# Two-layer hybrid decoder on one core: the MLP's order written down for all engines one step ahead, its first 1024 features multiplied plainly, PSUM banks in two kinds

## The chip, the cores and the metric

The kernel runs on one core of one Trainium2 chip. The metric is the device time of one execution in microseconds (us). A core has TensorE (PE) for matmuls and transposes, VectorE (DVE), ScalarE (ACT) and GpSimd (POOL) for the rest, and SyncE (SP), which here does nothing but issue transfers of weights. Matmuls write into PSUM, which has eight banks of 128 partitions x 2 KB (one 128x512 fp32 tile each).

## The reference

256 tokens of width 2048 go through two layers. Each layer normalizes, projects to queries, keys, values and memory queries, does attention (layer 0 differential, layer 1 dilated in three groups) and attention over 256 memory tokens, projects out and adds, and then runs a squared-ReLU MLP:

```python
hm = _rmsnorm(x, g_mlp[i])
x = x + jnp.square(jax.nn.relu(hm @ w_mlp1[i])) @ w_mlp2[i]   # 2048 -> 8192 -> 2048
```

All is fp32. A final RMSNorm ends it.

## The kernel before

**Products.** A product of two fp32 matrices is made of three passes: each operand is split into hi (ACT, L114) and lo (DVE, L115, source minus hi), and PE adds hi·hi, hi·lo and lo·hi in one PSUM bank. Each weight tile (512 KB, 128 partitions x 1024 fp32) so costs one transfer on SP's queue (L82), one ACT and one DVE instruction of 1024 wide. `weights` (L106 to L117) does that with three buffers for raw tiles (RAW = 3) and four each for hi and lo.

**Stages of a layer.** Attention comes first: `gemm_feat` (queries and keys, two heads at a time, L126) is followed by scores, softmax parts on DVE and ACT and transposes (`tp`, L428) of these two heads; then `project_v` (`psv`) and `mix_out` (L534: `o`, `os`, transposes `op`, L558). Then comes the output projection (`pso`, L577 to L589), which also makes, chunk by chunk, the combined activations of the MLP (`to_comb`, L186), and then the MLP.

**The MLP.** The 8192 features are 8 blocks of 1024. Up: with two halves of the tokens, two halves of a 256-row slice of the weights and two halves of the block's features it is a 2x2 times 2x2 product, done by Winograd's seven products instead of eight. A step of it is one of 8 row slices (`kp`): `up_weights` (L207) loads two tiles b and o (L220, L222), makes from them the seven weight factors (s, o and t sums on DVE at L227, L229, L230, splits on ACT and DVE), and 21 matmuls (L602 to L604) add to seven banks p1 to p7. After eight steps one ACT and seven DVE instructions (L621 to L628) put the seven banks together, and Relu and Square (L630, L631) make `u`. `to_hT` (L635) transposes u (`pu`, L642, four tiles of four transposes) and splits it into hT. Down: `mlp_down` (L651) has 4 column pieces n with four weight tiles (`raw_d`) each, and for each of two token halves t a group of 24 matmuls into one bank `psd` (L669 to L671); ACT scales it to `part` (L674) and POOL adds it to x in SBUF by an accumulating DMA (L675). The last block of a layer adds on DVE (L677) instead; in layer 0 it also transposes the new x for the next layer (`to_feat`, `pt_xa`, L176).

**What sets the order.** In the MLP PE's order is written by hand (`manual_schedule` for PE alone): first all of block 0's up steps and one of block 1; then for each block c, hT of c within up step 1 of block c+1, and the eight down groups of c, each followed by an up step of c+1 (the last by step 0 of c+2). Everything else (ACT, DVE, SP, POOL in the MLP, and all engines outside it) is ordered by a planner that simulates the program.

**PSUM banks.** `bank` (L72 to L74) has two tags: "u" of 7 banks in rotation, for all gemms, for scores, transposes and the seven products; and "d", one bank, for `pu` and `psd` of the MLP.

Of the kernel before, what the change touches and what calls it, by code (L numbers as in the profile page):

```python
# [9 lines left out]
F32 = mybir.dt.float32  # L10
# [7 lines left out]
P = 128  # L18
S = 256
D = 2048  # L20
KT = D // P
# [18 lines left out]
PRODUCTS = ("p1", "p2", "p4", "p5", "p6", "p3", "p7")  # L40
# [18 lines left out]
def trunk(ctx: ExitStack, tc: tile.TileContext, x, mem, g_attn, w_in, w_out, lambda_qk,  # L59
# [10 lines left out]
    psum = ctx.enter_context(tc.tile_pool(name="psum", bufs=7, space=bass.MemoryType.PSUM))  # L70
# [31 lines left out]
    pw = bank([P, 512], "pw")  # L102
# [23 lines left out]
    def gemm_feat(w, acts, nm, raws=(None,) * 4):  # L126

        ps = [bank([P, 2, 256], f"ps_{nm}_{j}") for j in range(2)]
# [57 lines left out]
    def to_comb(kp, gcol, nm):  # L186
# [3 lines left out]
        for a in range(2):  # L190
            k = 2 * kp + a
            for t in range(2):
                nc.tensor.transpose(pt[:, a, t, :], x_sb[:, t, k * P:(k + 1) * P], ident)
            nc.scalar.activation(xs[:, a], pt[:, a], AF.Copy, scale=gT[:, gcol + k:gcol + k + 1])
        cs = work.tile([P, 4, P], F32, tag="tmp", bufs=TMP, name=f"cs_{nm}")
        a11, a12, a21, a22 = xs[:, 0, 0], xs[:, 1, 0], xs[:, 0, 1], xs[:, 1, 1]
# [5 lines left out]
        cb = apool.tile([P, 7, 2, P], F32R, tag="act", name=f"cb_{nm}")  # L202
        for i0, i1, a in ((0, 2, xs[:, :, 0]), (2, 3, xs[:, 1, 1:2]), (3, 7, cs)):
            split(cb[:, i0:i1, 0, :], cb[:, i0:i1, 1, :], a)
        return cb

    def up_weights(w, kp, f0, nm):  # L207

# [13 lines left out]
        nc.sync.dma_start(o, pair(512, -512))  # L222
        b11, b22 = pieces(b, 2, "b")
        oh = upool.tile([P, 2, 512], F32R, tag="up", bufs=UP, name=f"oh_{nm}")
        split(oh[:, 0], oh[:, 1], o[:, 1])
        s = upool.tile([P, 2, 512], F32, tag="ut", bufs=UT, name=f"s_{nm}")
# [5 lines left out]
        return {"p1": b11, "p2": (oh[:, 0], oh[:, 1]), "p3": b22, "p5": t1, "p7": t3, "p6": t2, "p4": t4}  # L232
# [73 lines left out]
    def project_mem():  # L306
        mrstd = rstd_of(mssq, "mem")
        mrowb = bcast_row(mrstd, "mem")
        for i in range(DEPTH):
# [4 lines left out]
            ps = [bank([P, 512], f"psvm{i}_{t}") for t in range(2)]  # L314
# [120 lines left out]
    for i in range(DEPTH):  # L435
# [89 lines left out]
        def project_v(g):  # L525
            ps = [bank([P, 512], f"psv{i}{g}_{t}") for t in range(2)]
# [50 lines left out]
        for c in range(4):  # L577
            ps = [bank([P, 512], f"pso{i}{c}_{t}") for t in range(2)]
# [19 lines left out]
        turns = []  # L598

        def product(ps, n, kp, hi, lo):  # L600
            ah, al = (comb[kp][:, PRODUCTS.index(n), h, :] for h in range(2))
            nc.tensor.matmul(ps, ah, hi, start=kp == 0, stop=False)  # L602
            nc.tensor.matmul(ps, ah, lo, start=False, stop=False)  # L603
            nc.tensor.matmul(ps, al, hi, start=False, stop=kp == KP - 1)  # L604

        def mlp_up(c):


            nm = f"{i}{c}"
            ps = {n: bank([P, 512], f"{n}_{nm}") for n in ("p1", "p3", "p2", "p5", "p7", "p6", "p4")}  # L610
            for kp in range(KP):
                wt = up_weights(w_mlp1[i], kp, c * 1024, f"{nm}{kp}")
                for n in ps:
                    if turns and n in ("p1", "p3", "p5", "p6"):
                        next(turns[0])
                    product(ps[n], n, kp, *wt[n])
                if kp < KP - 1:
                    yield
            c1, u2, u3, u4 = (work.tile([P, 512], F32, tag="tmp", bufs=TMP, name=f"t{n}_{nm}") for n in range(4))
            c11, m12, c21, m22 = (work.tile([P, 512], F32, tag="ev", bufs=EV, name=f"u{n}_{nm}") for n in range(4))  # L620
            nc.scalar.activation(c1, ps["p1"], AF.Copy)  # L621
            nc.vector.tensor_tensor(u2, c1, ps["p6"], op=ALU.subtract)
            nc.vector.tensor_tensor(c11, c1, ps["p2"], op=ALU.add)
            nc.vector.tensor_tensor(u4, u2, ps["p5"], op=ALU.add)
            nc.vector.tensor_tensor(u3, u2, ps["p7"], op=ALU.add)
            nc.vector.tensor_tensor(m12, u4, ps["p3"], op=ALU.add)
            nc.vector.tensor_tensor(m22, u3, ps["p5"], op=ALU.add)
            nc.vector.tensor_tensor(c21, u3, ps["p4"], op=ALU.add)  # L628
            for u, sign in ((c11, 1.0), (m12, -1.0), (m22, -1.0), (c21, 1.0)):
                nc.scalar.activation(u, u, AF.Relu, scale=sign)  # L630
                nc.scalar.activation(u, u, AF.Square)  # L631
            ublk[c] = ((c11, 0, 0), (m12, 0, 1), (c21, 1, 0), (m22, 1, 1))
            yield

        def to_hT(c):  # L635
# [3 lines left out]
            for n, (u, t, f) in enumerate(ublk[c]):  # L639
                pt = bank([P, 4, P], f"pu_{i}{c}{n}", True)  # L640
# [6 lines left out]
        final = i == DEPTH - 1  # L647
        ssq = small.tile([P, 2, 4], F32, tag="ssq", name=f"ssq_e{i}")
        nxt = []

        def mlp_down(c):  # L651


            for n in range(3 if final and c == NC - 1 else 4):
                if final and c == NC - 1:
# [3 lines left out]
                wt = []  # L659
                xc = x_sb[:, :, n * 512:(n + 1) * 512]  # L660
                for t in range(2):
                    ps = bank([P, 512], f"psd{i}{c}{n}{t}", c < NC - 1)
                    for k in range(8):
                        r0 = c * 1024 + k * P
                        if k == len(wt):
                            wt += weights(w_mlp2[i][r0:r0 + 256, n * 512:(n + 1) * 512], 2, 512, f"d{i}{c}{n}{k}")
                        hi, lo = wt[k]
                        ah, al = (hT[k // 4][:, k % 4, h, t * P:(t + 1) * P] for h in range(2))
                        nc.tensor.matmul(ps, ah, hi, start=k == 0, stop=False)  # L669
                        nc.tensor.matmul(ps, ah, lo, start=False, stop=False)  # L670
                        nc.tensor.matmul(ps, al, hi, start=False, stop=k == 7)  # L671
                    if c < NC - 1:
                        part = work.tile([P, 512], F32, tag="tmp", bufs=TMP, name=f"part{i}{c}{n}{t}")
                        nc.scalar.activation(part, ps, AF.Copy, scale=rsq[:, t:t + 1])  # L674
                        nc.gpsimd.dma_start(xc[:, t, :], part, accum_op=ALU.add)  # L675
                    else:
                        nc.vector.scalar_tensor_tensor(xc[:, t, :], ps, rsq[:, t:t + 1], xc[:, t, :],  # L677
                                                       op0=ALU.mult, op1=ALU.add)
                    yield
                if c == NC - 1:  # L680
                    if not final:
                        xt = act_tile(f"xT{i + 1}_{n}")
                        to_feat(lambda t: x_sb[:, t, :], n, xt, (i + 1) * KT, f"xa{i}{n}")
                        nxt.append(xt)
                    for t in range(2):
                        sumsq(xc[:, t, :], ssq[:, t, n:n + 1])
                    if final:
                        for t in range(2):
                            nc.vector.tensor_tensor(xc[:, t, :], xc[:, t, :], gf, op=ALU.mult)

        with tc.manual_schedule(engines={mybir.EngineType.PE}):
            ups = [mlp_up(c) for c in range(NC)] + [iter(()), iter(())]
            for _ in ups[0]:
                pass
            next(ups[1])
            for c in range(NC):
                turns.append(to_hT(c))
                next(ups[c + 1], None)
                for _ in turns.pop():
                    pass  # L700
                for k, _ in enumerate(mlp_down(c)):
                    next(ups[c + 1] if k < 6 else ups[c + 2] if k == 6 else iter(()), None)
# [70 lines left out]
```

## Time and profile before

| | us |
|---|---|
| median of 3 runs | 2617.06 (2615.62 to 2618.43) |
| profiled execution, its own time | 2610.07 |
| its span in the trace | 2608.3 |

Times in rows are us from the start of the span. A row of a timeline gives the start, the duration, engine, line, operation, output and inputs by name; "x4" is four in a row; the bracket is the engine's idle time before it and what ended it. "Wait" rows sum such idle time by the pair of waiting and releasing line. PEclk is the granted TensorE clock as a share of full speed (2.4 GHz). Of a DMA, "to landing" is the time from its issue on the queue to its completion.

### The profile page before, as it was taken

Reading aid. Unit: us, or ns where it says so; the run is one execution under the profiler, and the core shown is the slowest. Engines: PE = TensorE matmul, PEld = TensorE weight load, DVE = VectorE, ACT = ScalarE, POOL = GpSimd, SP = SyncE. Lnnn points to the kernel's source line nnn. Section 1 sums busy time; section 2 is a strip of 40 time slices with the busy share of each in tenths; the row PEclk is TensorE's granted clock in tenths of the full one; section 3 lists DMA queues with packets and bytes.
Section 4 is the critical chain, followed back from the end, with each engine's and each line's share of the span. In section 5 each row is a group of like instructions: output and inputs, shape, how many; then the busy total and the mean of one; then the engine's idle time right before and its main releaser. Section 6 shows DMA issues by size and latency. Waiting matters only on the chain.

```text
span 2608.3 us, 28509 instructions
## 1 busy us (share of the span) xinstructions
PE 2294.7 (88%) x10310; PEld 1845.6 (71%) x10310; DVE 1780.9 (68%) x2194; ACT 1355.7 (52%) x1890; POOL 114.5 (4%) x146
## 2 busy tenths in 40 slices
PE   9977678698899999999977888989798999999997
PEld 7856556575678778777866677777477787787776
DVE  6544554468887888788754344456888878978874
ACT  6433333355565666566544333445456656656563
POOL 0000000000000000000000000000000000000000
PEclk9978788899999999999998888999999999999998
DMA  7633344454476667667644244555466766776664
GB/s 230 193 106 105 97 122 129 130 185 145 140 216 200 190 210 217 200 190 213 174 141 145 91 131 130 165 188 185 121 175 189 217 199 207 215 203 188 202 174 145
DMA packets 262400, 443.51 MB, mean 170 GB/s; under 512 B 14497, under 2 KB 80242, under 8 KB 262002
## 3 DMA queue, kind: packets, MB, share of 16 engines
q1 hardware_dynamic: 245856, 412.14, 50.3%
q0 software_dynamic: 16128, 29.37, 6.3%
q8 instruction: 81, 1.33, 0.2%
q14 instruction: 61, 0.50, 0.1%
q10 hardware_dynamic: 274, 0.17, 0.0%
HBM read 409.12 MB, written 3.15 MB: 158 GB/s over the span
## 4 chain that ended last, share of the span: by engine, by line
PE 39%; DVE 20%; DMA 13%; issue 7%; ACT 5%; POOL 0%; SPq 0%; DVEq 0%; POOLq 0%; ACTq 0%
DMA raw_d<-in_w_mlp_dram 6%; DMA o<-in_w_mlp_dram 6%; PE psd L669 4%; PE psd L670 4%; PE psd L671 3%; DVE lo_d L115 3%; PE p L602 3%; PE p L603 3%; PE p L604 3%; DVE b L230 2%; DVE b L229 2%; ACT hi_d L114 2%; DVE sl L115 2%; DVE bl L115 2%; PE ps_q L143 2%
## 5 line engine op out<-in xcount | busy, mean ns | idle before, releaser
L669 PE MATMUL psd<-hi_d,hT 128*128 128x512 f32 x1008 | 396.0, 393 | 8.0 <-DVE hT L115 6.4
L670 PE MATMUL psd<-lo_d,hT 128*128 128x512 f32 x1008 | 393.8, 391 | 1.0 <-DVE lo_d L115 1.0
L671 PE MATMUL psd<-hi_d,hT 128*128 128x512 f32 x1008 | 393.3, 390 | 0.0
L114 ACT ACTIVATE hi_d<-raw_d 128x1024 fp32r<-128x1024 f32 x252 | 260.2, 1053 | 198.8 <-DMA raw_d<-in_w_mlp_dram 104.6
L115 DVE TENSOR_TENSOR lo_d<-raw_d,hi_d 128x1024 fp32r<-128x1024 f32 x252 | 307.0, 1223 | 75.4 <-ACT hi_d L114 73.7
L114 ACT ACTIVATE th<-b 128x1024 fp32r<-128x1024 f32 x128 | 135.3, 1057 | 209.0 <-DVE b L230 198.4
L669 PEld LDWEIGHTS psd<-hi_d,hT 128*128 128x128 f32 x1008 | 190.2, 189 | 54.5 <-DVE hT L115 12.4
L670 PEld LDWEIGHTS psd<-lo_d,hT 128*128 128x128 f32 x1008 | 190.0, 188 | 40.5 <-DVE lo_d L115 1.7
L671 PEld LDWEIGHTS psd<-hi_d,hT 128*128 128x128 f32 x1008 | 189.9, 188 | 39.8
L115 DVE TENSOR_TENSOR bl<-b,bh 128x1024 fp32r<-128x1024 f32 x128 | 156.0, 1219 | 73.6 <-ACT bh L114 73.6
L227 DVE TENSOR_TENSOR s<-b,o 128x1024 f32<-128x1024 f32 x128 | 156.4, 1222 | 72.1 <-DMA o<-in_w_mlp_dram 71.3
L115 DVE TENSOR_TENSOR tl<-b,th 128x1024 fp32r<-128x1024 f32 x128 | 156.4, 1222 | 54.9 <-ACT th L114 54.0
L143 PE MATMUL ps_q<-xT,hi_q 128*128 128x512 f32 x384 | 158.5, 446 | 0.0
L115 DVE TENSOR_TENSOR sl<-s,sh 128x1024 fp32r<-128x1024 f32 x128 | 155.8, 1217 | 2.9 <-ACT sh L114 1.6
L675 POOL DMA_DIRECT2D x_sb<-part x112 | 97.3, 869 | 1333.7 <-ACT part L674 1322.7
L114 ACT ACTIVATE sh<-s 128x1024 fp32r<-128x1024 f32 x128 | 134.8, 1053 | 28.1 <-PE p L603 27.3
L114 ACT ACTIVATE bh<-b 128x1024 fp32r<-128x1024 f32 x128 | 135.0, 1054 | 26.7 <-PE p L603 24.5
L143 PE MATMUL ps_k<-xT,hi_k 128*128 128x512 f32 x384 | 136.2, 397 | 0.0
L115 DVE TENSOR_TENSOR lo_k<-raw_k,hi_k 128x1024 fp32r<-128x1024 f32 x48 | 58.7, 1223 | 109.7 <-ACT hi_k L114 109.7
L674 ACT ACTIVATE part<-psd,rsq 128x512 f32<-128x512 f32 x112 | 76.3, 681 | 98.9 <-PE psd L671 98.7
L603 PE MATMUL p<-tl,cb_xm 128*128 128x512 f32 x256 | 103.7, 405 | 22.7 <-DVE tl L115 22.5
L642 PE MATMUL pu<-ident,u 128*128 128x128 f32 x256 | 51.0, 332 | 74.6 <-DVE hT L115 56.6
(322 smaller groups left out, 5161.0 us busy)
## 6 DMA issues: line engine op xcount, KB each, us to landing
raw_d<-in_w_mlp_dram SPq DMA_DIRECT2D x252, 512.0 KB, 5.6
b<-in_w_mlp_dram SPq DMA_DIRECT2D x128, 512.0 KB, 5.5
o<-in_w_mlp_dram SPq DMA_DIRECT2D x128, 512.0 KB, 3.7
x_sb<-part POOLq DMA_DIRECT2D x112, 256.0 KB, 6.6
raw_q<-in_w_in_dram SPq DMA_DIRECT2D x48, 512.0 KB, 3.6
raw_k<-in_w_in_dram SPq DMA_DIRECT2D x48, 512.0 KB, 3.5
raw_v<-in_w_in_dram SPq DMA_DIRECT2D x48, 512.0 KB, 3.6
raw_o<-in_w_out_dram SPq DMA_DIRECT2D x48, 512.0 KB, 3.6
```

The source lines that it names most:

```text
L114: nc.scalar.activation(dst_hi, src, AF.Copy)
L115: nc.vector.tensor_tensor(dst_lo, src, dst_hi.bitcast(F32), op=ALU.subtract)
L143: nc.tensor.matmul(ps[j].rearrange("p h t -> p (h t)"), hi[:, cols], a.rearrange("p h t -> p (h t)"), **f)
L227: nc.vector.tensor_tensor(s, b, o[:, 0:1].to_broadcast([P, 2, 512]), op=ALU.add)
L602: nc.tensor.matmul(ps, ah, hi, start=kp == 0, stop=False)
L603: nc.tensor.matmul(ps, ah, lo, start=False, stop=False)
L604: nc.tensor.matmul(ps, al, hi, start=False, stop=kp == KP - 1)
L669: nc.tensor.matmul(ps, ah, hi, start=k == 0, stop=False)
L670: nc.tensor.matmul(ps, ah, lo, start=False, stop=False)
L671: nc.tensor.matmul(ps, al, hi, start=False, stop=k == 7)
L674: nc.scalar.activation(part, ps, AF.Copy, scale=rsq[:, t:t + 1])
L675: nc.gpsimd.dma_start(xc[:, t, :], part, accum_op=ALU.add)
```

## The change

1. PSUM: two tags of 4 banks each, "m" for gemms (projections, `pso`, the plain block, p1, p2, p5, p7, and the last block's `psd`) and "a" for all else (scores, all transposes, p3, p6, p4, the other `psd`).
2. Block 0 of each layer's MLP is multiplied plainly (`up_plain`: 16 weight tiles, 12 matmuls each). For it `to_comb` keeps one more factor (a21), and its three splits become two.
3. In the MLP from block 1 on, the order of all engines is the order of the program. The weights of an up step are made one step ahead (`prep_up` for step g+2 stands between the matmuls of step g+1 and group g), those of a down piece in two halves after each second step, b and o are used as before but sums go into o and s stands first. `to_hT` is taken in turns with the matmuls of one step and with that step's `prep`; a block's end (`end_up`) stands before the group g = 6, its last two Relu and Square behind it.
4. The last block's `mlp_down` (`last_down`) stands outside the hand-written order; its `to_hT` within it.

```diff
-    def bank(shape, nm, lone=False):
-        return psum.tile(shape, F32, tag="d" if lone else "u", bufs=1 if lone else 7, name=nm)
+    def bank(shape, nm, gemm=False):        # pool of 4 per tag
+        return psum.tile(shape, F32, tag="m" if gemm else "a", name=nm)
...
     def to_comb(kp, gcol, nm):
-        cb = apool.tile([P, 7, 2, P], F32R, tag="act", name=f"cb_{nm}")
-        for i0, i1, a in ((0, 2, xs[:, :, 0]), (2, 3, xs[:, 1, 1:2]), (3, 7, cs)):
-            split(cb[:, i0:i1, 0, :], cb[:, i0:i1, 1, :], a)
+        cb = apool.tile([P, 8, 2, P], F32R, tag="act", name=f"cb_{nm}")
+        split(cb[:, 0:4, 0, :], cb[:, 0:4, 1, :], xs.rearrange("p t a c -> p (t a) c"))
+        split(cb[:, 4:8, 0, :], cb[:, 4:8, 1, :], cs)
...
     def up_weights(w, kp, f0, nm):          # after the DMAs of b and o:
+        nc.vector.tensor_tensor(s, b, o[:, 0:1].to_broadcast([P, 2, 512]), op=ALU.add)
+        yield
         b11, b22 = pieces(b, 2, "b")
-        split(oh[:, 0], oh[:, 1], o[:, 1])
-        nc.vector.tensor_tensor(s, b, o[:, 0:1].to_broadcast([P, 2, 512]), op=ALU.add)
-        t1, t3 = pieces(s, 2, "s")
-        nc.vector.tensor_tensor(b[:, 0], s[:, 0], b[:, 1], op=ALU.add)
-        nc.vector.tensor_tensor(b[:, 1], b[:, 0], o[:, 1], op=ALU.add)
-        t2, t4 = pieces(b, 2, "t")
+        yield
+        nc.vector.tensor_tensor(o[:, 0], s[:, 0], b[:, 1], op=ALU.add)
+        split(oh[:, 0], oh[:, 1], o[:, 1])
+        nc.vector.tensor_tensor(o[:, 1], o[:, 0], o[:, 1], op=ALU.add)
+        t1, t3 = pieces(s, 2, "s")
+        t2, t4 = pieces(o, 2, "t")
...
+        def up_plain():
+            u = {}
+            for f in range(2):
+                ps = [bank([P, 512], f"pu0_{i}{f}{t}", True) for t in range(2)]
+                for kp in range(KP):
+                    wt = weights(w_mlp1[i][kp * 256:(kp + 1) * 256, f * 512:(f + 1) * 512], 2, 512, f"u0{i}{f}{kp}")
+                    for a in range(2):
+                        for t in range(2):
+                            passes(ps[t], comb[kp][:, 2 * t + a], *wt[a], kp == a == 0, kp == KP - 1 and a == 1)
+                for t in range(2):
+                    u[t, f] = work.tile([P, 512], F32, tag="ev", bufs=EV, name=f"u0_{i}{f}{t}")
+                    squared(u[t, f], ps[t], 1.0)
+            ublk[0] = [(u[t, f], t, f) for t in range(2) for f in range(2)]
...
+        def end_up(c):
+            nc.scalar.activation(c1, ps["p1"], AF.Copy)
+            # DVE c11, u2; squared(c11); DVE u4, m12; squared(m12); DVE u3, m22, c21
+            yield
+            squared(m22, m22, -1.0)
+            squared(c21, c21, 1.0)
...
-        with tc.manual_schedule(engines={mybir.EngineType.PE}):
-            ups = [mlp_up(c) for c in range(NC)] + [iter(()), iter(())]
-            for _ in ups[0]:
-                pass
-            next(ups[1])
-            for c in range(NC):
-                turns.append(to_hT(c))
-                next(ups[c + 1], None)
-                for _ in turns.pop():
-                    pass
-                for k, _ in enumerate(mlp_down(c)):
-                    next(ups[c + 1] if k < 6 else ups[c + 2] if k == 6 else iter(()), None)
+        up_plain()
+        with tc.manual_schedule():
+            run(prep_up(1, 0))
+            step_up(1, 0)
+            run(prep_up(1, 1))
+            prep_down(0, 0, (0, 1))
+            for c in range(NC - 1):
+                for g in range(8):
+                    uc, kp = (c + 1, g + 1) if g < 7 else (c + 2, 0)
+                    pc, pk = (c + 1, g + 2) if g < 6 else (c + 2, g - 6)
+                    prep = prep_up(pc, pk) if pc < NC else iter(())
+                    if g == 0:
+                        step_up(uc, kp, to_hT(c), prep)
+                    elif uc < NC:
+                        step_up(uc, kp)
+                    run(prep)
+                    ending = end_up(c + 1) if g == 6 else iter(())
+                    next(ending, None)
+                    n, t = g // 2, g % 2
+                    more = (c, n + 1) if n < 3 else (c + 1, 0)
+                    if t == 1:
+                        prep_down(*more, (0,))
+                    add_down(c, n, t, group_down(c, n, t, False))
+                    run(ending)
+                    if t == 1:
+                        prep_down(*more, (1,))
+            run(to_hT(NC - 1))
+        last_down(NC - 1)
```

`prep_down(c, n, halves)` issues two weight tiles of a down piece per half (load, hi, lo), `group_down` the 24 matmuls and `add_down` the `part` and the accumulating DMA, as before. The buffer counts (RAW, WH, UX, UT, UP) are unchanged, and so is the number of ACT, DVE and PE instructions of an up step and of a down group.

## Rows read from the trace of the kernel before

**Rows 1.** The page's span and its busy time of each engine.
```profile
span 2608.3 us, 28509 instructions
PE 2294.7 (88%) x10310; PEld 1845.6 (71%) x10310; DVE 1780.9 (68%) x2194; ACT 1355.7 (52%) x1890; POOL 114.5 (4%) x146
```

**Rows 2.** Busy time by stretch; the columns are the stretch, its length, then busy us (and instructions) of PE, PEld, DVE, ACT and POOL, the granted PE clock, the DMA share and GB/s. The stretches are, of layer 0: attention, output projection, the MLP up to the first down group, from there to the first down group of block 6, block 6, and block 7's down groups; of layer 1: attention, and the MLP up to the first down group.
```profile
132.80:510.50 377.70, 273.66 (x1333) 224.20 (x1332) 179.82 (x305) 134.83 (x252) 6.04 (x6) 0.83 0.38 116
510.50:604.40 93.90, 92.75 (x410) 75.00 (x408) 55.46 (x82) 49.37 (x75) 0.00 (x0) 0.98 0.54 168
604.40:690.80 86.40, 64.35 (x235) 42.60 (x235) 75.42 (x98) 47.57 (x68) 0.69 (x1) 0.94 0.42 123
690.80:1247.80 557.00, 520.47 (x2256) 418.69 (x2256) 462.22 (x498) 341.54 (x415) 41.74 (x48) 0.98 0.70 204
1247.80:1334.00 86.20, 76.33 (x334) 62.11 (x335) 63.31 (x72) 46.48 (x57) 10.34 (x18) 0.95 0.58 162
1334.00:1390.00 56.00, 49.40 (x226) 40.04 (x224) 29.61 (x36) 25.83 (x43) 0.00 (x0) 0.98 0.41 127
1418.10:1730.90 312.80, 265.56 (x1284) 219.18 (x1283) 143.50 (x195) 121.12 (x199) 0.00 (x0) 0.87 0.44 133
1823.40:1909.50 86.10, 65.00 (x235) 43.52 (x234) 75.38 (x98) 47.41 (x68) 0.70 (x1) 0.92 0.42 124
```

**Rows 3.** PE's waits in the attention stage of layer 0 (132.8 to 510.5): total us, how many, the longest.
```profile
PE tp L428 <- DVE e L496: 51.6, 12, 4.6
PE op L558 <- DVE os L555: 29.2, 6, 6.9
PE sc L487 <- DVE qk L271: 10.4, 6, 1.8
PE pTp_m L406 <- DVE e_m L402: 10.0, 4, 2.7
```

**Rows 4.** The same of layer 1 (1418.1 to 1730.9).
```profile
PE tp L428 <- ACT e L422: 15.4, 12, 1.6
PE pTp_m L406 <- DVE e_m L402: 10.4, 4, 3.1
PE sc L432 <- DVE qk L271: 10.4, 6, 1.8
PE op L558 <- DVE os L555: 8.1, 6, 2.1
```

**Rows 5.** DVE's split of the first weight tile of the third pair of heads' queries, and PE's instructions in order of time around it.
```profile
304.18 1.22 DVE L115 TENSOR_TENSOR lo_q<-raw_q,hi_q 128x1024 fp32r<-128x1024 f32 x1
...
309.91 0.45 PE L428 MATMUL tp<-ident,e 128*128 128x128 f32 x1 [4.57 <-DVE e L496]
...
316.57 0.45 PE L428 MATMUL tp<-ident,e 128*128 128x128 f32 x1 [4.02 <-DVE e L496]
316.67 0.77 PE L143 MATMUL ps_q<-xT,hi_q 128*128 128x512 f32 x1
```

**Rows 6.** PE at two following matmuls of the MLP, and at a tile of `pu` and the matmul behind it.
```profile
757.54 0.39 PE L602 MATMUL p<-bh,cb_xm 128*128 128x512 f32 x1
757.77 0.39 PE L603 MATMUL p<-bl,cb_xm 128*128 128x512 f32 x1
...
771.72 0.66 PE L642 MATMUL pu<-ident,u 128*128 128x128 f32 x4 [1.19 <-ACT part L674]
772.13 0.47 PE L602 MATMUL p<-bh,cb_xm 128*128 128x512 f32 x1
```

**Rows 7.** DVE in a stretch of the MLP where it did not wait between instructions.
```profile
658.25 1.23 DVE L227 TENSOR_TENSOR s<-b,o 128x1024 f32<-128x1024 f32 x1 [0.30 <-DMA o<-in_w_mlp_dram]
659.39 0.69 DVE L115 TENSOR_TENSOR oh<-o,oh 128x512 fp32r<-128x512 f32 x1
660.00 0.68 DVE L229 TENSOR_TENSOR b<-s,b 128x512 f32<-128x512 f32 x1
```

**Rows 8.** ACT in a stretch of the MLP.
```profile
754.42 0.61 ACT L114 ACTIVATE oh<-o 128x512 fp32r<-128x512 f32 x1
754.94 1.05 ACT L114 ACTIVATE sh<-s 128x1024 fp32r<-128x1024 f32 x1
755.89 0.61 ACT L630 ACTIVATE u<-u 128x512 f32<-128x512 f32 x1
```

**Rows 9.** PE's waits in layer 0's MLP (690.8 to 1309).
```profile
PE pu L642 <- DVE hT L115: 16.6, 12, 2.3
PE pu L642 <- ACT part L674: 8.8, 6, 2.5
PE p L603 <- DVE tl L115: 6.6, 6, 1.1
```

**Rows 10.** The transfers of raw down weights on the page: count, KB each, median us from issue to landing; and the spread of the landings of the same in 690.8 to 1309.
```profile
raw_d<-in_w_mlp_dram SPq DMA_DIRECT2D x252, 512.0 KB, 5.6
DMA to landing us min/median/max: 3.7/5.6/8.1
```

**Rows 11.** What SP's queue waited for ahead of the loads of raw tiles in 690.8 to 1309: total us, how many, the longest.
```profile
SPq L82 <- DVE lo_d L115: 163.0, 108, 11.1
```

**Rows 12.** PE at one of the four tiles of `pu` of layer 0's last block, and at the first `pt_xa`.
```profile
1330.74 1.12 PE L642 MATMUL pu<-ident,u 128*128 128x128 f32 x4 [1.41 <-DVE hT L115]
...
1348.07 0.98 PE L176 MATMUL pt_xa<-ident,x_sb 128*128 128x128 f32 x7 [1.65 <-DVE x_sb L677]
```

More of the change, by code (lines that the diff above doesn't have):

```diff
@@ L101, in trunk @@
     nc.vector.memset(zero, 0.0)
-    pw = bank([P, 512], "pw")
+    pw = bank([P, 512], "pw", True)
     for n in range(NWARM):
@@ L126, in gemm_feat @@
     def gemm_feat(w, acts, nm, raws=(None,) * 4):
-        ps = [bank([P, 2, 256], f"ps_{nm}_{j}") for j in range(2)]
+        ps = [bank([P, 2, 256], f"ps_{nm}_{j}", True) for j in range(2)]
         for pc in range(4):
@@ L313, in project_mem @@
                             f"km{i}{c}")
-            ps = [bank([P, 512], f"psvm{i}_{t}") for t in range(2)]
+            ps = [bank([P, 512], f"psvm{i}_{t}", True) for t in range(2)]
             for c in range(4):
@@ L525, in project_v @@
         def project_v(g):
-            ps = [bank([P, 512], f"psv{i}{g}_{t}") for t in range(2)]
+            ps = [bank([P, 512], f"psv{i}{g}_{t}", True) for t in range(2)]
             c0 = 2 * MIXW + g * 512
@@ L577, in trunk @@
         for c in range(4):
-            ps = [bank([P, 512], f"pso{i}{c}_{t}") for t in range(2)]
+            ps = [bank([P, 512], f"pso{i}{c}_{t}", True) for t in range(2)]
             for n, g in enumerate(("m", 0, 1, 2)):
@@ L597, in trunk @@
         ublk = {}
[L598 to L618, printed above, removed]
+        final = i == DEPTH - 1
@@ new lines, in trunk, with passes, squared @@
+        ssq = small.tile([P, 2, 4], F32, tag="ssq", name=f"ssq_e{i}")
+        nxt = []
+        def passes(ps, acts, hi, lo, first, last):
+            nc.tensor.matmul(ps, acts[:, 0, :], hi, start=first, stop=False)
+            nc.tensor.matmul(ps, acts[:, 0, :], lo, start=False, stop=False)
+            nc.tensor.matmul(ps, acts[:, 1, :], hi, start=False, stop=last)
+        def squared(u, src, sign):
+            nc.scalar.activation(u, src, AF.Relu, scale=sign)
+            nc.scalar.activation(u, u, AF.Square)
@@ new lines, in trunk, with prep_up, step_up @@
+        banks, facts, dw = {}, {}, {}
+        def prep_up(c, kp):
+            making = up_weights(w_mlp1[i], kp, c * 1024, f"{i}{c}{kp}")
+            for _ in range(2):
+                next(making)
+                yield
+            facts[c, kp] = next(making)
+        def step_up(c, kp, turns=None, prep=None):
+            if kp == 0:
+                banks[c] = {n: bank([P, 512], f"{n}_{i}{c}", n in ("p1", "p2", "p5", "p7")) for n in facts[c, 0]}
+            for n, (hi, lo) in facts.pop((c, kp)).items():
+                if turns and n in ("p1", "p3", "p5", "p6"):
+                    next(turns)
+                    if n in ("p1", "p5"):
+                        next(prep)
+                passes(banks[c][n], comb[kp][:, FACTORS.index(n)], hi, lo, kp == 0, kp == KP - 1)
@@ L619, in mlp_up @@
+        def end_up(c):
+            nm, ps = f"{i}{c}", banks.pop(c)
             c1, u2, u3, u4 = (work.tile([P, 512], F32, tag="tmp", bufs=TMP, name=f"t{n}_{nm}") for n in range(4))
@@ L639, in to_hT @@
             for n, (u, t, f) in enumerate(ublk[c]):
-                pt = bank([P, 4, P], f"pu_{i}{c}{n}", True)
+                pt = bank([P, 4, P], f"pu_{i}{c}{n}")
                 for k in range(4):
@@ L645, in to_hT, with prep_down, group_down, add_down @@
                 yield
[L647 to L655, printed above, removed]
+        def prep_down(c, n, halves):
+            for h in halves:
+                for k in (4 * h, 4 * h + 2):
+                    r0 = c * 1024 + k * P
+                    dw[c, n, k], dw[c, n, k + 1] = weights(w_mlp2[i][r0:r0 + 256, n * 512:(n + 1) * 512], 2, 512,
+                                                           f"d{i}{c}{n}{k}")
+        def group_down(c, n, t, gemm):
+            ps = bank([P, 512], f"psd{i}{c}{n}{t}", gemm)
+            for k in range(8):
+                passes(ps, hT[k // 4][:, k % 4, :, t * P:(t + 1) * P], *dw[c, n, k], k == 0, k == 7)
+            return ps
+        def add_down(c, n, t, ps):
+            part = work.tile([P, 512], F32, tag="tmp", bufs=TMP, name=f"part{i}{c}{n}{t}")
+            nc.scalar.activation(part, ps, AF.Copy, scale=rsq[:, t:t + 1])
+            nc.gpsimd.dma_start(x_sb[:, t, n * 512:(n + 1) * 512], part, accum_op=ALU.add)
+        def last_down(c):
+            for n in range(3 if final else 4):
+                xc = x_sb[:, :, n * 512:(n + 1) * 512]
+                if final:
                     gf = work.tile([P, 512], F32, tag="tmp", bufs=TMP, name=f"gf{n}")
@@ L658, in mlp_down @@
                                                   ap=[[0, P], [1, 512]]))
-                wt = []
-                xc = x_sb[:, :, n * 512:(n + 1) * 512]
+                if n:
+                    prep_down(c, n, (0, 1))
                 for t in range(2):
[L662 to L684, printed above, removed]
-                    for t in range(2):
[L686 to L689, printed above, removed]
@@ new lines, in last_down @@
+                    nc.vector.scalar_tensor_tensor(xc[:, t, :], ps, rsq[:, t:t + 1], xc[:, t, :],
+                                                   op0=ALU.mult, op1=ALU.add)
+                if not final:
+                    xt = act_tile(f"xT{i + 1}_{n}")
+                    to_feat(lambda t: x_sb[:, t, :], n, xt, (i + 1) * KT, f"xa{i}{n}")
+                    nxt.append(xt)
+                for t in range(2):
+                    sumsq(xc[:, t, :], ssq[:, t, n:n + 1])
+                if final:
+                    for t in range(2):
+                        nc.vector.tensor_tensor(xc[:, t, :], xc[:, t, :], gf, op=ALU.mult)
@@ new lines, in run @@
+        def run(steps):
+            for _ in steps:
+                pass
+        up_plain()
[25 more added lines that the diff above has]
+            run(to_hT(NC - 1))
```

28 lines of the change are left out of this document (14 added, 14 removed).

## Prediction

> **What bounds the kernel now.** I began with the page's busy times: PE is busy for 88% of the span and DVE for 68% [rows 1], so PE sets the time where it is fed, and the question is where it isn't. The table by stretch answers that [rows 2]. In the output projection PE is busy 92.75 of 93.9 us: nothing to gain. In the attention stages it is busy 273.7 of 377.7 us and 265.6 of 312.8, at a granted clock of 0.83 and 0.87. In the MLP's first part it is busy 64 of 86 us while DVE is busy 75: there DVE is the bound, in each layer. In the long middle part six blocks take 557.0 us, 92.8 each.
>
> The waits say what PE lacks. In attention it is the softmax chain of the heads [rows 3, 4]: the four largest waits add up to 101.2 us in layer 0 and 44.3 in layer 1. What follows such a wait matters more: the first weight tile of the next pair's queries was split at 304.2, yet PE idled 4.57 and 4.02 us for the heads' transposes and began the query gemm at 316.67, right behind the last head's first transpose [rows 5]. The gemm came behind the wait in PE's order although its data were there. In the MLP's middle PE waits for `hT`, `part` and `tl`, 32 us in six blocks [rows 9].
>
> **Unit prices.** One 512-column matmul takes 0.23 us of PE and a tile of `pu` 0.41 [rows 6], so an up step (21) 4.8 us, a down group (24) 5.4, a pair of each 20.4, a block with its 16 short transposes 83.3. DVE takes 1.14 us per 1024-wide and 0.61 per 512-wide instruction [rows 7], ACT 0.95 and 0.52 [rows 8]. An up step costs DVE four of the first and three of the second, 6.4; a down piece 4.6; two steps and a piece 17.3; a block with seven instructions of `end_up` and four `hT` 75.8. So PE, not DVE, is the floor of a middle block.
>
> **First 1024 features plain.** Removed: eight up steps of DVE (51 us), the bound there; PE's 168 matmuls become 192. Added: 16 weight tiles, 16 x 1.14 = 18 us of DVE, all beside PE's 192 x 0.227 = 43.5 us, which is now the bound; the tiles' transfers hide too, since three raw buffers at 3.7 us [rows 10] plus 2.1 of splits give one per 2 us against 2.7 of PE. Then, up to the first down group, DVE has two preps, a piece and four `hT`: 12.7 + 4.6 + 2.4 = 19.7, with about 3 of first transfer in front: 22.8. Sum 66.3 instead of 86.4: **-20 per layer**. Two splits of four factors instead of three: nothing, ACT and DVE being half idle in the output projection [rows 2].
>
> **Middle blocks.** The new order fixes DVE and SP too. A down piece has four raw tiles but there are three buffers, so the fourth load waits on SP until DVE has done lo of the first; before, SP waited in the same way [rows 11], but the planner let other work go past. Now b and o of the next two steps stand behind that load on SP's queue, and on DVE the next step's `s` stands behind the fourth lo. Walk a pair, with time 0 where lo of tile 0 starts: it ends at 1.2, the fourth load is issued at 1.3 and lands at 5.9 (I take 4.6 us, between the least of 3.7 and the median of 5.6 [rows 10]: fewer transfers are under way at once); hi ends at 6.9, so lo starts at 7.0 instead of 3.4. `s` waits for o, third in that line, until 8.7 (each 512 KB behind another adds about 1.4 us; an estimate from the spread of these landings, 3.7 to 8.1 over three places). It would have begun at 4.6. The pair lasts 17.3 + 4.1 = 21.4 on DVE, more than PE's 20.4: DVE becomes the pace.
>
> At a turn between blocks two pairs grow. With `end_up`: + 7 x 0.6 = 4.2 on DVE and 2.4 because the next step's bh stands behind Relu and Square on ACT: 28. With `hT`: each of the four tiles is transposes 0.41, hi 0.6, lo 0.68 [rows 6 to 8], in a row, since p3, p6 and p4 hold three of the four "a" banks: 6.7 on top: 28.1. PE idles there for the banks and for `hT`. A block is 2 x 21.4 + 2 x 28.1 = 99 against 92.8: **+6.2, six times per layer**. With a landing of 3.7 the pair is PE's 20.4 and the block 94.5; with 5.6 it is 103.
>
> Moved with no cost of their own: the POOL accumulations (POOL is idle nine tenths of the time [rows 2]); `s` ahead of the splits, as DVE must do both before `tl`.
>
> The traced transfers decide the landing; a page prices it lower. By the Trainium skill, DMA: Bandwidth & Descriptors, Anatomy of one DMA, a transfer costs about 2.0 us and its bytes at 436 GB/s, for its GpSimd path; 512 KB would be 3.2 us, an estimate from that page, below any landing in these rows. By it the pairs would be PE's, a block 94 and the total about 2475.
>
> **Last block.** Before, block 6 with the last `hT` took 86.2 [rows 2], its four `pu` tiles in turn in one bank with 1.4 us idle between [rows 12]. After, more banks are free there, but the last `hT` still stands bare: 8 groups and 6 steps are 72.1 of PE, DVE's pace adds about 3, the four `hT` 6.7: 81.8, **-4.5 per layer**. In layer 0 the `pt_xa` transposes waited for the addition on DVE, 1.65 us at the first of four [rows 12]; with gemm banks of their own, the next piece's matmuls can go ahead: four times 2, with the transposes' own hand-over, **-8** once (nothing if the planner keeps the order).
>
> **Attention.** No instruction changes; only the bank a tile sits in. With one rotation for all, the next gemm's bank came after the banks of the heads' transposes in program order, and PE's order shows that [rows 5]. With a rotation of its own a gemm may pass them. What it can fill: at most the waits of [rows 3, 4], 146 us, and somewhat more as the granted clock would rise (PE's busy time at the output projection's 0.98 would be 232 and 236 us, so 146 and 77 us are free, 223 in all). At least: nothing, if the planner keeps its order. I take 100, two thirds of the waits: the waits for `op`, 37 us, have little gemm work left behind them, and each head's PE work queues behind up to some 5 us of gemm. Ends 0 and -160.
>
> **Sum,** against the profiled execution's 2610.07: 2 x (6 x 6.2 - 20 - 4.5) = +25; -8; -100: 2527. That execution was 7.0 below the median of the runs, so 2534 in its terms; I say **2535**. Own range of this case 2450 to 2600.
>
> **Rivals.**
> B, slower: the fourth raw load costs what I say, and attention is not filled (the planner's order does not hang on the banks, so the bank split does nothing there). For it: nothing in a profile shows that the planner uses a freedom. Against: [rows 5]. 2617 + 25 - 8 = 2634; with a landing of 5.6, 2682. It decides from a fill under 17 us.
> C, slower: four banks are too few for a kind: scores, transposes and `o` wait for their evacuation, as PE now waits up to 1.8 us for `qk` [rows 3, 4]; at some 12 places of 1.75 us, 21, with no fill: 2655. Against: no wait of now is one for a bank outside the MLP. The Trainium skill, Perfetto Trace Analysis, Identifying Performance Opportunities, has it that consistent bubbles can mean too little PSUM for the next tile; by that rule four banks where seven stood would add such bubbles, and no row here yet shows one outside the MLP.
> D, much faster: the fourth load hides (the DVE order leads PE by more than I walk), middle blocks run at PE's 83.3 to 85: 12 x 9 less than now instead of 12 x 6.2 more, so about 180 below my forecast: 2355 with the fill, 2455 without. Against: WH and RAW are unchanged and the walk has DVE wait each pair.
>
> **Chances.** Forecast 0.62, B 0.20, C 0.08, D 0.10. The range 2430 to 2660 holds the forecast with its bounds, B up to a landing of about 5.2, C, and the part of D without fill; some 0.15 is left out. A measurement of this kernel can tell about 0.2%, 5 us, from no change. Faster: 0.60 of the forecast and D, 0.70. Same: fills that just pay for the MLP, 0.06. Slower: the rest of B, and C, 0.24.
>
> **What would show it.** Right: PE's query gemms start before the heads' `tp`, waits of rows 3 halved, attention of layer 0 near 310 us and of layer 1 near 280; first part of the MLP 66 us; middle blocks 99, with PE waiting for factors, DVE for hi of the fourth tile and o, SP for lo. Wrong: attention as long as now (B), PE waiting for evacuations there (C), middle blocks below 88 (D), or the first part not PE-bound.

## The result and the profile after

The change made the kernel faster: 2528.5 us median (2525.97 to 2529.33) against 2616.34 (2614.53 to 2618.43), ratio 0.9662, 95% interval 0.9646 to 0.9679. The forecast was 2535. That the total came out is luck: two of its terms were wrong by some 117 us each, in opposite directions, and both lie outside the bounds that the prediction gave them.

The page of the changed kernel, to set beside [rows 1]:

```profile
span 2527.2 us, 28282 instructions
PE 2262.8 (90%) x10358; PEld 1842.7 (73%) x10358; DVE 1718.1 (68%) x2084; ACT 1334.0 (53%) x1840; POOL 115.8 (5%) x146
```

The table by stretch says where the time went (columns as in [rows 2]). For the changed kernel, layer 0: attention with the output projection, which overlap now; the MLP up to the first down group; six middle blocks; the last block's first part; its down groups. Layer 1: attention with the output projection; the MLP up to the first down group; six middle blocks.

```profile
131.00:468.50 337.50, 334.51 (x1742) 277.90 (x1741) 229.26 (x378) 181.04 (x320) 6.05 (x6) 0.99 0.56 172
468.50:538.10 69.60, 58.06 (x260) 47.07 (x258) 37.06 (x48) 34.55 (x48) 0.70 (x1) 0.93 0.55 167
538.10:1189.60 651.50, 546.49 (x2257) 433.66 (x2257) 471.15 (x499) 345.02 (x415) 41.77 (x48) 0.91 0.57 174
1189.60:1272.70 83.10, 75.09 (x335) 61.18 (x335) 62.30 (x70) 46.70 (x57) 11.54 (x18) 0.99 0.56 163
1272.70:1345.20 72.50, 72.50 (x354) 60.40 (x355) 45.92 (x62) 37.44 (x61) 0.71 (x1) 0.96 0.59 191
1345.20:1667.00 321.80, 321.80 (x1694) 274.76 (x1693) 197.51 (x269) 167.66 (x267) 0.00 (x0) 1.00 0.58 177
1667.00:1736.40 69.40, 57.87 (x260) 46.98 (x258) 37.05 (x48) 34.54 (x48) 0.70 (x1) 0.93 0.55 167
1736.40:2389.90 653.50, 549.65 (x2257) 435.95 (x2257) 471.34 (x499) 345.33 (x415) 41.72 (x48) 0.90 0.57 174
```

Of the kernel before, the two stretches that join its attention and output projection, and layer 1's six middle blocks:

```profile
132.80:604.40 471.60, 366.41 (x1741) 299.20 (x1739) 235.28 (x387) 184.20 (x327) 6.04 (x6) 0.86 0.41 126
1418.10:1823.40 405.30, 356.90 (x1694) 293.21 (x1693) 200.99 (x278) 170.56 (x274) 0.00 (x0) 0.90 0.47 144
1909.50:2466.80 557.30, 520.79 (x2257) 417.85 (x2257) 461.91 (x498) 340.52 (x415) 41.67 (x48) 0.98 0.70 204
```

| term, both layers | forecast | measured |
|---|---|---|
| attention with output projection | -100 | -134.1 - 83.5 = -217.6 |
| MLP up to the first down group | -40 | -16.8 - 16.7 = -33.5 |
| twelve middle blocks | +74 | +94.5 + 96.2 = +190.7 |
| block 6 with the last hT | -9 | -3.1 - 2.0 = -5.1 |
| last down groups of layer 0 | -8 | -11.6 |
| start and end of the program | 0 | -4.0 |
| sum | -83 | -81.1 |

In attention PE hardly waits any more: this is all that is left in layer 0, to set beside the 101 us of [rows 3], and layer 1 has no such line.

```profile
PE pso L162 <- ACT hi_o01m L114: 2.5, 1, 2.5
PE pso L163 <- DVE lo_o01m L115: 0.5, 1, 0.5
```

How that is done stands in PE's order of time (to compare with [rows 5]): the query gemm (`ps_q`) runs on both sides of the heads' transposes (`tp`) and scores (`sc`), without idle time.

```profile
247.81 0.28 PE L140 MATMUL ps_q<-xT,lo_q 128*128 128x256 f32 x1
247.93 0.27 PE L431 MATMUL tp<-ident,e 128*128 128x128 f32 x1
248.13 0.48 PE L490 MATMUL sc<-qk 64*128 64x128 f32 x2
248.54 0.44 PE L431 MATMUL tp<-ident,e 128*128 128x128 f32 x2
248.91 0.92 PE L490 MATMUL sc<-qk 64*128 64x128 f32 x6
249.76 0.50 PE L143 MATMUL ps_q<-xT,hi_q 128*128 128x512 f32 x1
```

In the middle blocks of layer 0 (538 to 1190) PE's waits answer to [rows 9]; the second list is DVE's:

```profile
PE pu L677 <- DVE hT L115: 39.0, 6, 7.0
PE p L606 <- ACT t L655: 34.7, 6, 7.0
PE p L607 <- DVE bl L115: 13.2, 6, 2.3
PE pu L677 <- ACT part L699: 12.7, 6, 2.7
```
```profile
DVE lo_d L115 <- ACT hi_d L114: 92.9, 33, 4.4
DVE s L226 <- DMA o<-in_w_mlp_dram: 40.5, 24, 3.0
```

Three of PE's lines, 86.4 us, stand at the turn between blocks, once per block; the one for `bl` stands in the third pair of each block. DVE's waits are spread wider: 24 waits for o in 24 pairs of steps. Here is one pair on DVE (its first three lo, the fourth, the next `s`, and the first lo of the next pair; this pair also holds `end_up`), then the fourth load, what follows it on SP and the accumulation that POOL issues at that time, and the hi on ACT that waits for the load:

```profile
706.30 3.50 DVE L115 TENSOR_TENSOR lo_d<-raw_d,hi_d 128x1024 fp32r<-128x1024 f32 x3
713.78 1.23 DVE L115 TENSOR_TENSOR lo_d<-raw_d,hi_d 128x1024 fp32r<-128x1024 f32 x1 [3.98 <-ACT hi_d L114]
716.99 1.23 DVE L226 TENSOR_TENSOR s<-b,o 128x1024 f32<-128x1024 f32 x1 [1.98 <-DMA o<-in_w_mlp_dram]
...
737.07 3.50 DVE L115 TENSOR_TENSOR lo_d<-raw_d,hi_d 128x1024 fp32r<-128x1024 f32 x3
```
```profile
707.54 0.37 SPq L82 DMA_DIRECT2D raw_d<-in_w_mlp_dram  x1
707.96 0.46 SPq L221 DMA_DIRECT2D b<-in_w_mlp_dram  x1
708.48 0.46 SPq L223 DMA_DIRECT2D o<-in_w_mlp_dram  x1
708.98 0.47 SPq L221 DMA_DIRECT2D b<-in_w_mlp_dram  x1
709.50 1.01 SPq L223 DMA_DIRECT2D o<-in_w_mlp_dram  x1
...
707.99 0.85 POOL L700 DMA_DIRECT2D x_sb<-part  x1 [7.91 <-ACT part L699]
```
```profile
712.69 1.06 ACT L114 ACTIVATE hi_d<-raw_d 128x1024 fp32r<-128x1024 f32 x1 [4.14 <-DMA raw_d<-in_w_mlp_dram]
```

This is the walk of the prediction line by line: first lo, then the load 1.24 us later (walked 1.3), 5.1 us until hi can start (4.6), the fourth lo 7.5 after the first (7.0), and `s` 10.7 after it (8.7).

### The profile page after: what moved, and what is told of

It reads as the page before. It is cut to its first block, busy times and chain, and to the rows that moved or that the text cites. A ratio compares the mean times of both kernels' runs of the same rounds, so it can differ in the third digit from the quotient of the medians.

```text
span 2527.2 us, 28282 instructions
## 1 busy us (share of the span) xinstructions
PE 2262.8 (90%) x10358; PEld 1842.7 (73%) x10358; DVE 1718.1 (68%) x2084; ACT 1334.0 (53%) x1840; POOL 115.8 (5%) x146
## 4 chain that ended last, share of the span: by engine, by line
PE 53%; DVE 16%; DMA 16%; ACT 7%; issue 7%; SPq 1%; DVEq 0%; ACTq 0%; POOL 0%; POOLq 0%
DMA o<-in_w_mlp_dram 11%; DVE bl L115 4%; DMA raw_d<-in_w_mlp_dram 4%; PE ps_q L143 4%; PE ps_k L143 4%; ACT th L114 4%; PE psd L606 3%; PE psd L608 3%; PE psd L607 3%; DVE lo_d L115 3%; PE p L607 3%; PE p L606 2%; PE p L608 2%; PE pso L163 2%; PE pso L164 2%
## 5 line engine op out<-in xcount | busy, mean ns | idle before, releaser
L114 ACT ACTIVATE th<-o 128x1024 fp32r<-128x1024 f32 x112 | 118.8, 1061 | 196.7 <-DVE o L232 175.8
L226 DVE TENSOR_TENSOR s<-b,o 128x1024 f32<-128x1024 f32 x112 | 136.9, 1222 | 90.6 <-DMA o<-in_w_mlp_dram 90.6
L115 DVE TENSOR_TENSOR bl<-b,bh 128x1024 fp32r<-128x1024 f32 x112 | 136.8, 1221 | 87.8 <-ACT bh L114 87.8
L606 PE MATMUL p<-bh,cb_xm 128*128 128x512 f32 x224 | 105.1, 469 | 70.4 <-ACT t L655 66.6
L677 PEld LDWEIGHTS pu<-ident,u 128*128 128x128 f32 x256 | 36.6, 172 | 149.3 <-DVE hT L115 114.7
L115 DVE TENSOR_TENSOR tl<-o,th 128x1024 fp32r<-128x1024 f32 x112 | 137.2, 1225 | 5.9 <-ACT th L114 0.3
L114 ACT ACTIVATE bh<-b 128x1024 fp32r<-128x1024 f32 x112 | 118.2, 1055 | 39.0 <-DMA b<-in_w_mlp_dram 32.8
L143 PE MATMUL ps_q<-xT,hi_q 128*128 128x512 f32 x384 | 138.4, 401 | 0.0
L115 DVE TENSOR_TENSOR sl<-s,sh 128x1024 fp32r<-128x1024 f32 x112 | 136.5, 1218 | 0.0
L607 PE MATMUL p<-bl,cb_xm 128*128 128x512 f32 x224 | 100.0, 446 | 31.3 <-DVE bl L115 31.3
```

The source lines that it names most:

```text
L114: nc.scalar.activation(dst_hi, src, AF.Copy)
L115: nc.vector.tensor_tensor(dst_lo, src, dst_hi.bitcast(F32), op=ALU.subtract)
L606: nc.tensor.matmul(ps, acts[:, 0, :], hi, start=first, stop=False)
L607: nc.tensor.matmul(ps, acts[:, 0, :], lo, start=False, stop=False)
L677: nc.tensor.transpose(pt[:, k], u[:, k * P:(k + 1) * P], ident)
```

## The experiments

**The banks alone.** The kernel before with the pool in two kinds; p1, p2, p5, p7 and all gemms in "m".

```diff
-        return psum.tile(shape, F32, tag="d" if lone else "u", bufs=1 if lone else 7, name=nm)
+        return psum.tile(shape, F32, tag="m" if gemm else "a", name=nm)
...
```

Expected: 

> The kernel before with the two kinds of banks alone; MLP order and first block as before. Theory (the banks fill the attention stages, by what the changed kernel's trace shows: attention with output projection 134 us shorter in layer 0, 84 in layer 1): 2616 - 218 = about 2400, PE without idle time in the attention stages. Rival (the freedom comes with the rest of the change, or four banks of a kind cost the MLP as much): above 2500.

Measured 2361.83 us, ratio 0.9027 (0.9003 to 0.905). Its attention of layer 0 and of layer 1, and the MLP's middle blocks of layer 0:

```profile
129.20:466.60 337.40, 334.90 (x1741) 277.97 (x1740) 229.82 (x385) 180.87 (x326) 7.79 (x6) 0.99 0.57 177
553.00:1113.90 560.90, 523.91 (x2256) 420.75 (x2256) 462.17 (x498) 341.17 (x415) 41.75 (x48) 0.97 0.70 203
1265.50:1587.20 321.70, 321.70 (x1693) 274.82 (x1692) 198.37 (x276) 167.35 (x273) 0.00 (x0) 1.00 0.59 182
```

The bank split by itself gives the whole gain in attention; middle blocks stay at 93.5. It beat the forecast by 38 us, 23 of them in block 6: it fell to 73.9 us in each layer, from the 86.2 of [rows 2] in layer 0 and from 84.3 in layer 1. The split changes one more thing: attention had the seven banks of the one rotation before, and now it has all eight. A single rotation of eight was not run, so no run by itself excludes that one bank more makes part of the gain.

**The banks undone.** The changed kernel with the one rotation of seven and the lone bank.

```diff
-        return psum.tile(shape, F32, tag="m" if gemm else "a", name=nm)
+        return psum.tile(shape, F32, tag="d" if lone else "u", bufs=1 if lone else 7, name=nm)
...
```

Expected: 

> The changed kernel with the one rotation of 7 banks and the lone bank again. Theory: the attention stages take as long as before the change, 218 us more: about 2745; the MLP's middle blocks stay at about 108 us. Rival (the middle blocks are slow because p3, p6, p4 hold three of the four banks that psd and pu share): middle blocks change by over 5 us.

Measured 2762.27 us, ratio 1.0557 (1.0532 to 1.0582): without the banks the change is a loss.

```profile
132.20:603.70 471.50, 368.13 (x1744) 300.41 (x1742) 234.90 (x380) 184.77 (x321) 6.04 (x6) 0.84 0.40 123
672.40:1324.10 651.70, 546.88 (x2256) 435.31 (x2256) 471.25 (x499) 344.95 (x415) 41.74 (x48) 0.91 0.57 174
```

Attention is as long as before (471.5 against 471.6), and the middle blocks are as slow as in the changed kernel (651.7 against 651.5): the two effects are apart, and going back to the old banks changes nothing in the second. The rival is only half tested by this: `pu` and `psd` have one bank here (the lone one), and in the changed kernel too one is left to them while p3, p6 and p4 are held. What that one bank costs shows further on, where the fourth load is set free.

**Two banks for gemms, six for the rest.** The edit is shown against the kernel of the first experiment (the kernel before with two kinds of banks); besides, p5 and p7 move to "a", so that p1 and p2 are left in "m".

```diff
-        return psum.tile(shape, F32, tag="m" if gemm else "a", name=nm)
+        return psum.tile(shape, F32, tag="m" if gemm else "a", bufs=2 if gemm else 6, name=nm)
...
```

Expected: 

> As e1 (the kernel before with two kinds of banks), but two banks for gemms and six for the rest. Theory (what counts is that gemms have a rotation of their own; with two banks each gemm waits for its predecessor's evacuation, some 1 to 2 us at each of 30 gemms and the projections): 2390 to 2430. Rival (gemms must have room to run ahead of the heads by a whole gemm): at least half of the 218 us is lost, above 2470.

Measured 2399.46 us, ratio 0.9175 (0.9158 to 0.9193), inside the theory's range: 38 us more than with four and four. So 217 of the 255 us come with a rotation of two banks for gemms, and 38 with two more in it. The 38 are lost around attention: layer 0's MLP begins at 492.5 us instead of 466.6, and from layer 0's last down groups to layer 1's MLP it takes 414.5 us instead of 399.4; middle blocks (92.9 and 93.2) and block 6 (73.9) are as in the first experiment. That gemms with two banks of their own keep most of the gain speaks for the shared order, and against the eighth bank, as the cause.

**Order written for PE alone.**

```diff
-        with tc.manual_schedule():
+        with tc.manual_schedule(engines={mybir.EngineType.PE}):
```

Expected: 

> The changed kernel with the MLP's order written down for PE alone, so that the planner orders ACT, DVE and SP. Theory (the written order on DVE and SP makes a middle block 108.6 us instead of 92.8): 12 x 15.8 = 190 us less, about 2340. Rival (the slow middle blocks come from the bank kinds): 2500 to 2530.

Measured 2309.25 us, ratio 0.8829 (0.8809 to 0.885). Layer 0's middle blocks take 93.1 us each, and the part up to the first down group 64.4:

```profile
468.80:533.20 64.40, 57.92 (x259) 46.99 (x257) 39.54 (x50) 36.49 (x49) 0.70 (x1) 0.97 0.60 174
533.20:1091.90 558.70, 520.29 (x2257) 422.29 (x2257) 467.91 (x499) 351.05 (x414) 41.76 (x48) 0.97 0.70 203
```

So the written order of the engines other than PE cost 219 us, and the rest of the change, taken together, gains 307. The forecast of about 2340 is beaten by 31 because the order cost outside the middle blocks too: block 6 takes 73.9 and 74.0 us here, against 83.1 and 82.3, and the first part 5 less in each layer.

**The fourth load set free.** Which part of that order? The fourth raw tile of a down piece goes into a buffer of b and o, where each pair of steps uses four of five.

```diff
+        if spare:
+            raw = upool.tile([P, 2, 512], F32, tag="ux", bufs=UX, name=f"raw_{nm}").rearrange("p k c -> p (k c)")
...
+                    raw = load_weights(src, 2, 512, f"d{i}{c}{n}{k}", True) if k == 6 and c < NC - 1 else None
```

Expected: 

> The changed kernel, but the fourth raw tile of a down piece lies in one of the five buffers of b and o (one of five is spare there), so its load need not wait for lo of the first tile. Theory (DVE loses about 6 us in each pair of steps to that load, so 17.3 becomes 23.4 and the two turn pairs 30.8): ordinary pairs at PE's 20.4, turn pairs 24.8, a block 90.5 instead of 108.6: 12 x 18 = 217 less, about 2310. Rival (the turn's own chain of hT tiles through one bank, and c1 behind DVE, cost the time): only the fifth step's 3.5 us goes, 2470 to 2490.

Measured 2335.48 us, ratio 0.8926 (0.8906 to 0.8946), 25 above the theory's number. With the order otherwise untouched, middle blocks fall from 108.6 to 93.9:

```profile
535.70:1099.10 563.40, 525.03 (x2258) 422.94 (x2257) 469.31 (x499) 343.50 (x415) 41.75 (x48) 0.96 0.68 202
```

The theory asked for 90.5; the turn kept 3 us more. But the rival is out: of PE's 105.0 us of idle time in these six blocks 38.4 are left (36.5 before the change), so what the change had added, most of it at the turn, was made by a wait that stands in every pair. Counted from the starts of its down groups, PE took 20.5 and 20.7 us for a block's first two pairs in the changed kernel, since factors made ahead fed it, while DVE took 22.7 and 24.2; what DVE had lost came due at the turn.

**hT ahead of the fourth tile at the turn.**

```diff
-                    if t == 1:
+                    if t == 1 and g < 7:
                         prep_down(*more, (1,))
...
                         step_up(uc, kp, to_hT(c), prep)
+                        if c:
+                            run(prep)
+                            prep_down(c, 0, (1,))
...
```

Expected: 

> The changed kernel, but at each turn between blocks the second half of the next piece's weights (raw2, raw3 with hi and lo) stands behind the four hT tiles instead of ahead of them, in all engines' order. Theory (the fourth load's wait stands in front of hT on ACT and DVE; moved behind, it has landed by then): about 6 us less per middle block, 2528 - 72 = 2456. Rival (group 0 of the block then waits for lo of these tiles just as long): 2515 to 2530.

Measured 2483.16 us, ratio 0.95 (0.9479 to 0.9521). Layer 0's middle blocks take 102.9 us, 5.7 less, as the theory had it; layer 1's gain was 4.5, and each layer's block 6 got about 4 to 5 us longer, so the total is 45 less and not 72 (the traced execution was 7 us below this kernel's median).

**The two waits of a pair, one at a time.** First the accumulating DMAs of `part` taken out, so that this kernel leaves out that part of the result; then b and o of the next step (`fetch`) issued ahead of raw2 and raw3.

```diff
-            nc.gpsimd.dma_start(x_sb[:, t, n * 512:(n + 1) * 512], part, accum_op=ALU.add)
```

Expected: 

> The changed kernel without the accumulating DMAs of part into x (the down results of blocks 0 to 6 of each layer are left out; part is still made). Theory (the accumulation of 256 KB that POOL issues just behind the fourth raw load shares the transfer engines with it, b and o, and is why o lands 9.4 us after that load instead of the 7.4 walked): o lands about 1.8 us earlier, s waits that much less in each pair, a middle block is 5 to 7 us shorter, 2445 to 2470. Rival (the loads alone fill the line, the accumulation is hidden): 2515 to 2530.

```diff
+                        if fc < NC:
+                            fetch(fc, fk)
                         prep_down(*more, (1,))
...
```

Expected: 

> The changed kernel with b and o of the next up step issued ahead of the piece's raw2 and raw3 on SP instead of behind them; nothing else moves. Theory (two waits stand in each pair on DVE, 4 us of lo for the fourth tile and 2 of s for o; this takes the second away): 2 us less per pair, middle blocks about 100 to 102 instead of 108.7, 2430 to 2455. Rival (the fourth load then lands later by what the b and o gained): 2510 to 2530.

Measured 2466.39 us (ratio 0.9432, 0.9418 to 0.9446) and 2448.12 us (0.9368, 0.9348 to 0.9388), both totals in the theories' ranges. Without the accumulations layer 0's middle blocks take 104.0 us, 4.6 less, a little under the 5 to 7 that the theory asked for. Landings of o, in middle blocks of layer 0, of the changed kernel and without the accumulations:

```profile
DMA to landing us min/median/max: 8.7/10.2/11.0
```
```profile
DMA to landing us min/median/max: 8.1/8.4/9.1
```

These are landings of the second o of a pair; the trace has none for the first, the one that `s` waits for. But `s` tells the same: it starts 9.5 us after the fourth load is issued in the changed kernel and 7.8 without the accumulations (medians). One pair without them:

```profile
676.05 0.37 SPq L82 DMA_DIRECT2D raw_d<-in_w_mlp_dram  x1
...
683.66 1.23 DVE L226 TENSOR_TENSOR s<-b,o 128x1024 f32<-128x1024 f32 x1 [0.37 <-DMA o<-in_w_mlp_dram]
```

So the accumulation is what made o some 1.7 us later. With b and o first, DVE's waits for o disappear from its list and blocks fall to 102.4; the wait of lo for the fourth tile stays (88.5 us in 538 to 1120).

**The turn moved.** As the order for PE alone, but a block's last two groups stand behind its last up step, then its four `pu` tiles, and steps 3 and 4 follow each other (the line shown counts the groups behind step `kp`).

```diff
+                    for _ in range(0 if kp == 3 else 2 if kp == KP - 1 else 1):
...
```

Expected: 

> As e4 (PE's order alone written down), with another order: a block's last two groups stand behind its last up step, then the four pu tiles back to back, then step 0 of the next block; to make up for it two up steps follow each other in the middle (steps 3 and 4). Theory (what is left over PE's 83.3 us in a middle block of e4, about 9 us, stands at the turn: one bank for pu and psd, and end_up, hT and a new step in one short stretch): middle blocks 85 to 88 instead of 92.5, about 2230. Rival (DVE, busy 78 of 92 us, is late wherever the second of two steps stands): 2300 to 2330.

Measured 2291.53 us, ratio 0.8763 (0.8748 to 0.8779), the fastest kernel here. But the theory fell, and the time is not the rival's either (2300 to 2330): middle blocks of layer 0 take 92.4 us (from 93.1), and PE waits at the `pu` tiles for Square instead of for hT (600 to 1100):

```profile
PE pu L677 <- ACT u L612: 27.5, 11, 3.9
```

The MLP's first part takes 53.4 us instead of 64.4 in each layer, but not all of that is gain: the new order moves one up step from this stretch to block 6, which takes 78.5 us instead of 73.9.

```profile
470.70:524.10 53.40, 51.56 (x238) 42.31 (x237) 31.64 (x41) 31.85 (x44) 0.70 (x1) 1.00 0.61 180
1078.60:1157.10 78.50, 78.50 (x357) 65.24 (x355) 63.16 (x68) 49.97 (x59) 7.02 (x10) 1.00 0.60 171
```

So some 6.4 us are gained there in each layer. The same with the fourth tile in a buffer of b and o:

Expected: 

> As e6, with the fourth raw tile in a buffer of b and o as in e5. Theory (with the planner's order on DVE and SP the fourth load no longer stands in front of anything): within 5 us of e6. Rival (its wait still costs in each pair): 20 to 60 us less than e6.

Measured 2299.86 us, ratio 0.8795 (0.8779 to 0.8811), 8 us more than without: neither side's number, nearest the theory's. Where the planner orders DVE and SP, no cost of the fourth load shows. The blocks of both kernels stand some 9 us above PE's 83.3. In the first of the two 5.6 of them are idle time of PE and 3.5 are longer busy time, at a granted clock of 0.97; what would take away the idle time stays open.

## Why the prediction was right, and where it was wrong

**What bounds the kernel: right.** PE set the time, and the place to look was where a gemm stood behind a softmax in PE's order. That the one rotation of banks put it there was read from a single timeline [rows 5]; the first three experiments show it, but for the single rotation of eight banks that was not run.

**Attention: right in kind, sized at less than half.** The step that failed was "I take 100, two thirds of the waits". The reason for the cut was that the waits for `op` "have little gemm work left behind them": but the output projection goes past them, it starts at 367.2 us, while `op` runs from 352 to 411 and the stretch ends at 468.5. Idle time fell by 102 and 48 us, nearly all of it; and PE's busy time fell by 32 and 35 (366.4 to 334.5, 356.9 to 321.8) as the granted clock rose from 0.86 and 0.90 to 0.99 and 1.00, near the 2.4 GHz level. The sum, 217.6, is close to the "223 in all" that the text itself gave as free, and lies beyond its end of -160.

**First part: right.** 69.5 for 66.3. With PE's order alone written it is 64.4: in the written order of DVE hT stands behind the piece's last lo, and PE waits for it once per layer:

```profile
530.54 1.12 PE L677 MATMUL pu<-ident,u 128*128 128x128 f32 x4 [11.48 <-DVE hT L115]
```

**Middle blocks: right mechanism, sized at two fifths.** Forecast 99, measured 108.6 and 108.9. The pair's walk was 21.4 and 21.4, turns 28 and 28.1; measured on DVE, from first lo to first lo, 22.7, 24.2, 30.8 and 31.5. The failing step is the landing behind the fourth load: 5.1 us for 4.6, and o 9.4 for the 7.4 "third in that line". That line was not only SP's. The prediction let the POOL accumulations move "with no cost of their own" because POOL is idle; but the order puts one just behind the fourth load, and without them `s` starts 7.8 us after the load and a block takes 104.0. That is 4.6 of the 9.7 us missed per block; the other 5 are not traced to one cause. One thing the walk had no term for: of layer 0's 94.5 us, 26.0 are longer busy time of PE (546.5 against 520.5) at a granted clock of 0.91 instead of 0.98; how much of the 5 that makes is not shown. Twelve blocks times 9.7 are 116 us, by luck as much as attention gave beyond its forecast. (The walk's own lower bound, a landing of 3.7, adds up to 95.3 and not 94.5; nothing hangs on it.)

**Block 6.** The -4.5 per layer came from layer 0's 86.2 alone; layer 1's block took 84.3 before, so it gained 2.0 where layer 0 gained 3.1.

**The price of a load.** By the Trainium skill (DMA: Bandwidth & Descriptors, Anatomy of one DMA) 512 KB would take 3.2 us, an estimate from that page, and by it the pairs would have been PE's. The least landings of 512 KB in these traces come near it: 3.3 us for `raw_km`, ahead of attention in the changed kernel, with a median of 3.4. The loads that set the pairs do not: 5.1 with five more transfers issued within 2 us behind it, and over all raw tiles of layer 0's middle blocks 3.9 at the least and 9.8 in the median.

**Rivals.** B (no fill) and C (too few banks) are out by the first experiment; D by the middle blocks. For C the prediction named the Trainium skill (Perfetto Trace Analysis, Identifying Performance Opportunities), by which consistent bubbles can mean that there is too little PSUM for the next tile. The bubbles were in the kernel before, 101 us in [rows 3]; with four banks to a kind 3 us are left, and how the banks were handed out made most of the difference. The change mainly does two things that a sum alone could not tell apart: a gain of 218 and a loss of 191.

## What to carry to other kernels

Where long accumulations and short chains share one rotation of PSUM banks, give each a rotation of its own before writing any order by hand. When an order is written down for a queue, count for each buffer that is reloaded within a round what stands behind that load, and the transfers that other queues issue at that time: here POOL's made o 1.7 us later. And when an engine stands still at one place, look over the whole round of the engine that feeds it: PE stood still mostly at the turn, for a wait that DVE met in every pair.

## What was not expected

The size of one effect. PE's busy time for the same 1741 matmuls and transposes of layer 0's attention fell from 366.4 to 334.5 us once its gaps were filled, the granted clock rising from 0.86 to 0.99: filling 102 us of idle time gave back 134.
